# Value matmuls as side-by-side column tiles with VectorE sums in the last two tiles, and softmax reciprocals as powers of -1 on GpSimd

## The chip, the cores and the metric

The kernel runs on the eight NeuronCores of one Trainium2 chip, each core computing one of eight batch entries with the same program. The metric is the device time in microseconds of the slowest core. An execution is in a *fast* or a *slow* state: in the slow one the cores of one die or of both get a lower clock for TensorE and the time is some per cent longer, whatever the kernel. "Same" means a difference under 2%.

## The reference

A two-layer decoder trunk of width 1024 over 4096 positions. Each layer has a half-step SwiGLU feed-forward network (FFN), a mixing layer, and a second FFN. The mixing layer of layer 0 is a gated recurrence; that of layer 1 is causal attention with a learned forget gate, and both run 4 heads of cross-attention into 256 memory tokens beside it. The part that matters:

```python
s = jnp.einsum('bhqd,bhkd->bhqk', qb, k, preferred_element_type=F32) * scale
s = s + cb[..., None] - cum[:, :, None, :]
s = jnp.where(key_pos[None, :] <= q_pos[:, None], s, -jnp.inf)
p = jax.nn.softmax(s, axis=-1)
return jnp.einsum('bhqk,bhkd->bhqd', p.astype(v.dtype), v)
```

## The kernel before

The 4096 positions go in eight tiles of 512. A small scheduler inside the kernel runs at build time: it keeps a rough clock for every engine, books an assumed cost for each instruction, and picks greedily which piece of work is issued next, so attention, recurrence and norms are laid between the dense FFN matmuls. The order is then fixed; on the chip each engine takes its own queue strictly in that order and waits on semaphores. Attention of tile `t` has key blocks `0..4t+3` of 128 keys each. It does, per pair of heads and two key blocks, four score matmuls (64 rows each, two side by side), four exponentials on ScalarE, and four value matmuls whose stationary operand holds 64 columns of values and 64 columns of ones:

```python
for h2 in range(2):
    for i in range(2):
        blk = 2 * b + i
        p, q0 = ps_[2 * i + h2], q0s[i]
        self.mm(o[h2], o[h2].ap[:, q0:TT], vb.ap[:, blk % 8, h2:h2 + 2, :].rearrange("p a d -> p (a d)"),
                p.ap[:, q0:TT], blk == 0, blk == nkb - 1, [vb, p], signal=True)
```

The ones give the softmax denominator, copied 64 times, as the other half of the output. At the end of a head pair the denominators are inverted on VectorE in four pieces of 128 columns and multiplied with the values:

```python
def softmax_end(self, o, cat, c):
    dn, nu = self.F.get(), self.F.get()
    # ... four copies out of PSUM: values to nu, denominators to dn
    def recip(j):
        r = slice(128 * j, 128 * j + 128)
        self.fw.op("dve", lambda e, a=dn.ap[:, r]: e.reciprocal(a, a), reads=[dn], writes=[dn], cost=(None, 950.0))
    def end():
        cat[c] = self.Bp.get()
        self.tt("dve", cat[c], nu, dn, ALU.mult)
        self.F.put(dn, nu)
    return [(dn, lambda j=j: recip(j)) for j in range(4)] + [(nu, end)]
```

`cat` is what the output projection multiplies. `cost=(None, 950.0)` is what the scheduler books, in nanoseconds. The cross-attention of both layers uses the same ending, so there are (6 + 2) x 8 + 2 x 8 = 80 endings and 320 reciprocals.

## Time and profile before

| | before |
|---|---|
| time, two runs | 5461.5 us (fast), 5554.8 us (slow) |
| slowest core in the profile | 5459.7 us |
| TensorE on the chain that ended last | 87% |
| VectorE / ScalarE / GpSimd busy | 50% / 49% / 15% |
| mean granted TensorE clock | 0.98 to 0.99 |

The page cuts the span in 40 slices and gives the busy share of each in tenths. These are the rows of TensorE and GpSimd before:

```profile
PE   7898999999999999999999999999999999999999
...
POOL 1223120120211112210121012001200101001100
```

TensorE is nearly full from the second tenth on, and GpSimd has plenty of room. That room is what the second half of the change wants to use.

### The profile page before, as it was taken

Reading aid. Unit: us, or ns where it says so; the run is one execution under the profiler, and the core shown is the slowest. Engines: PE = TensorE matmul, PEld = TensorE weight load, DVE = VectorE, ACT = ScalarE, POOL = GpSimd, SP = SyncE. Lnnn points to the kernel's source line nnn. Section 1 sums busy time; section 2 is a strip of 40 time slices with the busy share of each in tenths; the row PEclk is TensorE's granted clock in tenths of the full one; section 3 lists DMA queues with packets and bytes.
Section 4 is the critical chain, followed back from the end, with each engine's and each line's share of the span. In section 5 each row is a group of like instructions: output and inputs, shape, how many; then the busy total and the mean of one; then the engine's idle time right before and its main releaser. Section 6 shows DMA issues by size and latency. Waiting matters only on the chain.

```text
span 5459.7 us, 84254 instructions; the slowest of 8 cores (5418.8 to 5459.7 us)
## 1 busy us (share of the span) xinstructions
PE 5252.4 (96%) x24835; PEld 2278.5 (42%) x24835; DVE 2730.0 (50%) x4101; ACT 2697.6 (49%) x4468; POOL 828.3 (15%) x1098
## 2 busy tenths in 40 slices
PE   7898999999999999999999999999999999999999
PEld 3443444444444443444434443444334444433344
DVE  4466643465545465635564455354544434443342
ACT  2356431344524365425672577246763656466641
POOL 1223120120211112210121012001200101001100
PEclk9999999999999997999999999999999999999999
DMA  8964687955795643455445443454435445555445
GB/s 180 218 170 126 143 207 175 224 141 169 167 223 181 181 127 112 147 162 146 137 134 174 144 140 115 138 169 134 135 112 189 146 146 158 184 158 169 152 148 161
DMA packets 302148, 866.23 MB, mean 159 GB/s; under 512 B 33680, under 2 KB 53264, under 8 KB 301712
## 3 DMA queue, kind: packets, MB, share of 16 engines
q1 hardware_dynamic: 275328, 775.47, 45.0%
q0 software_dynamic: 26384, 85.38, 10.3%
q8 instruction: 221, 3.62, 0.3%
q14 instruction: 215, 1.76, 0.1%
HBM read 819.72 MB, written 125.30 MB: 173 GB/s over the span
## 4 chain that ended last, share of the span: by engine, by line
PE 87%; DMA 5%; DVE 2%; ACT 2%; issue 2%; POOL 1%; SPq 1%; DVEq 0%; ACTq 0%; POOLq 0%
PE ps L652 87%; DMA sb_w<-wts 2%; DVE sb_f L686 1%; ACT sb_b L661 1%; DMA sb_f<-x 1%; ACT sb_f L661 1%; DMA wbf<-sb_w 1%; DVE sb_b L686 1%; SPq L221 1%; DMA sb_w<-wbf 1%; ACT L661 0%; POOL sb_f L669 0%; POOL sb_b L669 0%; DVE sb_b L669 0%; DVE sb_f L669 0%
## 5 line engine op out<-in xcount | busy, mean ns | idle before, releaser
L652 PE MATMUL ps<-sb_b,sb_w 128*128 128x512 bf16 x19728 | 4464.5, 383 | 83.9 <-DVE sb_f L686 27.0
L652 PEld LDWEIGHTS ps<-sb_b,sb_w 128*128 128x128 bf16 x19728 | 1909.2, 98 | 2513.6 <-issue 378.1
L661 ACT ACTIVATE sb_b<-ps,sb_nct 128x512 bf16<-128x512 f32 x1344 | 810.9, 691 | 342.6 <-PE ps L652 340.9
L661 ACT ACTIVATE sb_f<-ps 128x512 f32<-128x512 f32 x752 | 448.6, 597 | 1057.4 <-PE ps L652 1013.0
L686 DVE SCALAR_TENSOR_TENSOR sb_f<-sb_f,ps 128x512 f32<-128x512 f32 x704 | 481.4, 684 | 877.7 <-ACT sb_f L661 733.7
L686 DVE SCALAR_TENSOR_TENSOR sb_f<-ps,sb_f 128x512 f32<-128x512 f32 (+3 forms) x688 | 370.6, 574 | 889.0 <-PE ps L652 878.1
L669 DVE TENSOR_TENSOR sb_b<-sb_f,ps 128x512 bf16<-128x512 f32 x704 | 484.3, 688 | 287.8 <-PE ps L652 247.5
L669 POOL TENSOR_TENSOR sb_f<-sb_f 128x512 f32<-128x512 f32 (+1 forms) x282 | 360.9, 1280 | 1511.1 <-ACT sb_f L661 1506.7
L661 ACT ACTIVATE sb_f<-sb_f 128x512 f32<-128x512 f32 (+1 forms) x598 | 367.2, 625 | 415.3 <-DVE sb_f L686 248.2
L652 PE MATMUL ps<-sb_b,sb_vst 128*128 128x512 bf16 (+1 forms) x1728 | 428.9, 369 | 16.4 <-ACT sb_b L661 10.0
L669 POOL TENSOR_TENSOR sb_f<-sb_f,sb_cf 128x128 f32<-128x128 f32 x384 | 180.0, 485 | 1539.5 <-DVE sb_f L686 1532.8
L661 ACT ACT_TABLE_LOAD x172 | 220.7, 1283 | 227.4 <-PE ps L652 220.2
L661 ACT ACTIVATE sb_b<-sb_f,sb_nct 128x128 bf16<-128x128 f32 (+3 forms) x384 | 193.3, 555 | 243.6 <-POOL sb_f L669 242.7
L694 ACT COPY sb_f<-ps 128x512 f32<-128x512 f32 (+2 forms) x434 | 251.9, 582 | 114.7 <-PE ps L652 80.6
L962 DVE RECIPROCAL sb_f<-sb_f 128x128 f32<-128x128 f32 x320 | 302.2, 947 | 11.5 <-DVE sb_f L962 0.5
L686 DVE SCALAR_TENSOR_TENSOR sb_b<-sb_f,sb_vecs 128x512 bf16<-128x512 f32 (+1 forms) x392 | 286.4, 778 | 35.0 <-ACT sb_f L661 34.9
L652 PE MATMUL ps<-sb_b,sb_kst 64*128 64x512 bf16 (+1 forms) x1728 | 263.8, 368 | 22.8 <-DVE sb_f L686 9.0
L652 PEld LDWEIGHTS ps<-sb_b,sb_vst 128*128 128x128 bf16 x1728 | 160.4, 98 | 236.8 <-issue 79.7
L661 ACT ACTIVATE sb_b<-ps 128x512 bf16<-128x512 f32 (+1 forms) x258 | 143.1, 600 | 100.7 <-PE ps L652 100.5
L221 POOL DMA_DIRECT2D sb_w<-wts x179 | 97.0, 543 | 575.1 <-PE ps L652 446.6
L698 DVE COPY sb_f<-ps 64x512 f32<-64x512 f32 x160 | 109.7, 686 | 137.0 <-ACT sb_f L694 82.0
L669 DVE TENSOR_TENSOR sb_f<-ps,sb_f 128x512 f32<-128x512 f32 x128 | 88.5, 691 | 149.2 <-PE ps L652 149.2
(69 smaller groups left out, 1767.9 us busy)
## 6 DMA issues: line engine op xcount, KB each, us to landing
sb_w<-wbf SPq DMA_DIRECT2D x761, 512.0 KB, 4.1
sb_w<-wbf SPq DMA_DIRECT2D x424, 352.0 KB, 3.1
sb_w<-wts POOLq DMA_DIRECT2D x115, 512.0 KB, 9.6
wbf<-sb_w SPq DMA_DIRECT2D x113, 512.0 KB, 9.4
sb_vst<-vcache SPq DMA_DIRECT2D x96, 384.0 KB, 3.8
sb_kst<-kcache SPq DMA_DIRECT2D x96, 256.0 KB, 4.3
sb_w<-wts POOLq DMA_DIRECT2D x64, 352.0 KB, 9.6
wbf<-sb_w SPq DMA_DIRECT2D x64, 352.0 KB, 7.1
```

Source lines behind the costliest of these rows:

```text
L221: eng.dma_start(out=item[1], in_=item[2]).then_inc(item[3], 16)
L652: self.fw.op("pe", lambda e: e.matmul(out_ap, lhsT, rhs, start=start, stop=stop, skip_group_check=True), reads=reads, writes=[ps], signal= ...
L661: self.fw.op("act", lambda e: e.activation(o, i, func, **kw), reads=[in_b] + list(extra), writes=[out_b], cost=(func, ns))
L669: self.fw.op(eng, lambda e: e.tensor_tensor(o, a, b, op), reads=[a_b, b_b], writes=[out_b], cost=(None, 155 + 1.042 * n if eng == "dve" el ...
L686: self.fw.op("dve", lambda e: e.scalar_tensor_tensor(o, a, scalar, b, op0, op1), reads=[in0_b, in1_b] + list(extra), writes=[out_b], cost= ...
L694: fn, ns = (lambda e: e.copy(o, i)), 160 + 0.833 * n
L698: fn, ns = (lambda e: e.tensor_copy(o, i)), 155 + (1.042 if in_b.psum else 0.53) * n
L962: self.fw.op("dve", lambda e, a=dn.ap[:, r]: e.reciprocal(a, a), reads=[dn], writes=[dn], cost=(None, 950.0))
```

## The change

The intent is twofold. First, half of each value matmul is spent on ones. In the last two tiles (`SUMS = (6, 7)`), which are the longest, the ones go: the two heads' 64-column value matmuls run side by side in the two halves of the array, and VectorE adds the exponentials up itself. Second, VectorE then has more to do, so the reciprocals leave it, as `x ** -1` on GpSimd. The core of the diff, with cuts:

```diff
+    def inverse(self, b, r):
+        a = b.ap[:, r]
+        n = self.neg.ap.to_broadcast([128, self.width(a)])
+        self.fw.op("pool", lambda e: e.tensor_tensor(a, a, n, ALU.pow), reads=[b, self.neg], writes=[b], shared=True,
+                   cost=(None, 1500.0))
...
         def recip(j):
-            r = slice(128 * j, 128 * j + 128)
-            self.fw.op("dve", lambda e, a=dn.ap[:, r]: e.reciprocal(a, a), reads=[dn], writes=[dn], cost=(None, 950.0))
+            self.inverse(dn, slice(128 * j, 128 * j + 128))
...
+    def attn_sums(self, t, h, res, nxt):
...
+                        self.tt("dve", ac, p0, p, ALU.add, o=ac.ap[:, q0:TT], a=p0.ap[:, q0:TT], b=p.ap[:, q0:TT])
...
+                    self.mm(o, o.ap[64 * h2:64 * h2 + 64, q0:TT], vb.ap[:, blk % 8, 2 * h2, :], p.ap[:, q0:TT], blk == 0,
+                            blk == nkb - 1, [vb, p], signal=h2 == 1, tile=(128, 64, 0, h2))
...
+    SUMS = (6, 7)
```

The rest keeps the scheduler's books: eight places of the array in place of four, a model of the SBUF interface that VectorE and GpSimd share, other step counts. These alter the order of instructions from the first tiles on.

More of the change, by code (lines that the diff above doesn't have):

```diff
@@ L55, in reset @@
         self.free = 0.0
-        self.quad = [0.0] * 4
+        self.quad = [0.0] * 8
         self.mode = None
@@ L61, in reset @@
         self.busy = 0.0
+        self.port = collections.deque(maxlen=8)
 HOP = 100.0
@@ L120, in _deps, with _port, _run @@
         return at
-    def _run(self, q, at, cost):
+    def _port(self, q, at, ns):
+        for a, b in self.q["pool" if q.name == "dve" else "dve"].port:
+            if a - 50.0 <= at < b:
+                at = b
+        q.port.append((at, at + ns))
+        return at
+    def _run(self, q, at, cost, shared=False):
         if q.is_pe:
             n, rows, cols, r, c = cost
-            quads = [2 * i + j for i in ((0, 1) if rows == 128 else (r,)) for j in ((0, 1) if cols == 128 else (c,))]
+            w = cols // 32
+            quads = [4 * i + j for i in ((0, 1) if rows == 128 else (r,)) for j in range(w * c, w * c + w)]
             if (rows, cols) != q.mode:
-                before = max(q.quad) + (92.0 if q.mode else 0.0)
+                before = max(q.quad) + (100.0 if q.mode else 0.0)
             else:
@@ L148, in _run @@
             start += 1300.0
+        if shared:
+            start = self._port(q, start, ns)
         q.busy += ns
@@ L154, in pe_free, with op @@
         return max(self.q["pe"].quad)
-    def op(self, qname, fn, reads=(), writes=(), signal=True, cost=(None, 600.0)):
+    def op(self, qname, fn, reads=(), writes=(), signal=True, cost=(None, 600.0), shared=False):
         q = self.q[qname]
-        end = self._run(q, self._deps(q, reads, writes), cost)
+        end = self._run(q, self._deps(q, reads, writes), cost, shared)
         if signal:
@@ L293, in __init__ @@
         self.n = n
+        self.every = name[:4] != "attn"
         self.count = 0
@@ L345, in step @@
     def step(self, lane):
-        self.count += 1
+        self.count += 1 if lane.need.units or self.every else 0
         self.units += lane.need.units
@@ L512, in whole @@
         for k in range(8):
-            yield Need(self.h[k], f=2, lag=(("act", 700.0),))
+            yield Need(self.h[k], f=2, b=k // 7, lag=(("act", 700.0),))
             self.add(k)
@@ L572, in _tensors @@
         t["ones"] = sb("ones", [128, 128], F32)
+        t["neg"] = sb("neg", [128, 1], F32)
         t["vecs"] = sb("vecs", [128, self.vc["_n"]], F32)
@@ L605, in _bufs @@
         self.ones = B(t["ones"], "ones")
+        self.neg = B(t["neg"], "neg")
         self.vecs = B(t["vecs"], "vecs")
@@ L669, in tt @@
         self.fw.op(eng, lambda e: e.tensor_tensor(o, a, b, op), reads=[a_b, b_b], writes=[out_b],
-                   cost=(None, 155 + 1.042 * n if eng == "dve" else 190 + 2.11 * n))
+                   shared=eng == "pool" or not (a_b.psum or b_b.psum), cost=(None, 155 + 1.042 * n if eng == "dve" else 190 + 2.11 * n))
     def ts(self, eng, out_b, in_b, s1, s2, op0, op1, o=None, i=None, extra=()):
@@ L686, in stt @@
         self.fw.op("dve", lambda e: e.scalar_tensor_tensor(o, a, scalar, b, op0, op1),
-                   reads=[in0_b, in1_b] + list(extra), writes=[out_b], cost=(None, ns))
+                   reads=[in0_b, in1_b] + list(extra), writes=[out_b], shared=not (in0_b.psum or in1_b.psum), cost=(None, ns))
     def copy(self, eng, out_b, in_b, o=None, i=None):
@@ L698, in copy @@
             fn, ns = (lambda e: e.tensor_copy(o, i)), 155 + (1.042 if in_b.psum else 0.53) * n
-        self.fw.op(eng, fn, reads=[in_b], writes=[out_b], cost=(None, ns))
+        self.fw.op(eng, fn, reads=[in_b], writes=[out_b], shared=eng == "pool", cost=(None, ns))
     WRITE_AT = (1,)
@@ L884, in ffn @@
         if nxt:
-            yield Need(h[7], f=1)
+            yield Need(h[7], f=1, b=1)
             nxt.add(7)
@@ L1016, in out_proj @@
         if nxt:
-            yield Need(h[7], f=1)
+            yield Need(h[7], f=1, b=1)
             nxt.add(7)
@@ L1406, in attn, with load, drop, adds @@
         yield from self.out_proj(1, h, cat, nxt)
+    def attn_sums(self, t, h, res, nxt):
+        fw = self.fw
+        qT, qmn = res["q"][0:6], res["q"][6:8]
+        nkb = 4 * t + 4
+        nb = nkb // 2
+        chunks = [(c, j) for c in range(6) for j in range((nkb + 7) // 8)]
+        where = {x: i for i, x in enumerate(chunks)}
+        kv = {}
+        def load(i):
+            if i >= len(chunks):
+                return
+            c, j = chunks[i]
+            n = min(8, nkb - 8 * j)
+            kb, vb = self.kst.next(), self.vst.next()
+            tiles = range(2 * j, 2 * j + n // 4)
+            fw.dma("sp", kb.ap[:, 0:n * 128], self.kc_d[c, :, j * 1024:j * 1024 + n * 128],
+                   reads=[self.kc_bufs[(c, i)] for i in tiles], writes=[kb], kb=32 * n)
+            fw.dma("sp", vb.ap[:, 0:n].rearrange("p t a d -> p t (a d)"), self.vc_d[c, :, 8 * j:8 * j + n, :],
+                   reads=[self.vc_bufs[(c, i)] for i in tiles], writes=[vb], kb=48 * n)
+            kv[(c, j)] = (kb, vb)
+        load(0)
+        load(1)
+        cat = [None] * 8
+        pend, fins, live, factors, halves, scaled = [], [], {}, {}, {}, set()
+        state = {"qk": 0, "pv": 0, "done": 0}
+        sums, used = collections.deque(), collections.Counter()
+        def drop(pool, *bufs):
+            for x in bufs:
+                used[id(x)] += 1
+                if used[id(x)] == 2:
+                    del used[id(x)]
+                    pool.put(x)
+        def adds():
+            for _ in range(6 * nb):
+                yield Need(cond=lambda: bool(sums))
+                c, b, ps_, q0s = sums.popleft()
+                if b == 0:
+                    yield Need(f=2)
+                    acc = [self.F.get() for _ in range(2)]
+                elif b == 2 * t:
+                    for h2 in range(2):
+                        ec = factors[c][h2]
+                        yield Need(ec, lag=(("dve", self.LAG),))
+                        self.tt("dve", acc[h2], acc[h2], ec, ALU.mult)
+                        drop(self.F, ec)
+                for i in range(2):
+                    for h2 in range(2):
+                        p, q0, ac = ps_[2 * i + h2], q0s[i], acc[h2]
+                        if b == 0 and i == 0:
+                            continue
+                        p0 = ps_[h2] if b == 0 else ac
+                        yield Need(p, lag=(("dve", self.LAG),))
+                        self.tt("dve", ac, p0, p, ALU.add, o=ac.ap[:, q0:TT], a=p0.ap[:, q0:TT], b=p.ap[:, q0:TT])
+                        if b == 0 and q0:
+                            self.copy("dve", ac, p0, o=ac.ap[:, 0:q0], i=p0.ap[:, 0:q0])
+                        drop(self.Bp, p, *([p0] if b == 0 else []))
+                state["done"] += 1
+                if b == nb - 1:
+                    ends_of(c, acc)
+        def ends_of(c, x):
+            got = halves.setdefault(c, [])
+            got.append(x)
+            if len(got) == 2:
+                fins.append((c, *sorted(got, key=lambda y: isinstance(y, list))))
+        def scale(c):
+            o, ec = live[c], factors[c]
+            for h2 in range(2):
+                r = slice(64 * h2, 64 * h2 + 64)
+                self.tt("dve", o, o, ec[h2], ALU.mult, o=o.ap[r, :], a=o.ap[r, :], b=ec[h2].ap[r, :])
+            drop(self.F, *ec)
+            scaled.add(c)
+        def values(c, b, ps_, q0s, vb):
+            if b == 0:
+                live[c] = self.PS.get()
+            o = live[c]
+            for i in range(2):
+                blk, q0 = 2 * b + i, q0s[i]
+                for h2 in range(2):
+                    p = ps_[2 * i + h2]
+                    self.mm(o, o.ap[64 * h2:64 * h2 + 64, q0:TT], vb.ap[:, blk % 8, 2 * h2, :], p.ap[:, q0:TT], blk == 0,
+                            blk == nkb - 1, [vb, p], signal=h2 == 1, tile=(128, 64, 0, h2))
+            drop(self.Bp, *ps_)
+            state["pv"] += 1
+            if b == nb - 1 or b % 4 == 3:
+                load(where[(c, (2 * b) // 8)] + 2)
+            if b == nb - 1:
+                ends_of(c, live.pop(c))
+        def ripe():
+            c, b, ps_, _, vb = pend[0]
+            if b and b == 2 * t:
+                return False
+            now = fw.pe_free() - HOP
+            bufs = [*ps_, vb, *([live[c]] if b else ())]
+            return max(x.there() for x in bufs) <= now and (b > 0 or self.PS.room(5) <= now)
+        def products():
+            while state["pv"] < 6 * nb:
+                yield Need(cond=lambda: bool(pend) or state["pv"] == 6 * nb)
+                if not pend:
+                    continue
+                c, b, ps_, _, vb = pend[0]
+                if b and b == 2 * t and c not in scaled:
+                    scale(c)
+                n = int(b == 0)
+                yield Need(vb, *ps_, *([live[c]] if b else ()), ps=n, units=2)
+                if pend and pend[0][0:2] == (c, b):
+                    values(*pend.pop(0))
+        def scores():
+            for c in range(6):
+                cq = []
+                for b in range(nb):
+                    db = b - 2 * t
+                    if db == 0:
+                        ec = factors[c] = []
+                        for h2 in range(2):
+                            yield Need(self.c3, ps=1, f=2, lag=(("act", 1500.0),), units=1)
+                            x = self.PS.get()
+                            self.mm(x, x.ap, self.sel(2 * c + h2), self.c3.ap, True, True, [self.cb, self.c3])
+                            q = self.F.get()
+                            self.copy("act", q, x)
+                            cq.append(q)
+                            self.PS.put(x)
+                            if t > 0:
+                                e_ = self.F.get()
+                                self.act(AF.Exp, e_, q)
+                                ec.append(e_)
+                    while (c, (2 * b) // 8) not in kv:
+                        yield Need(cond=lambda: (c, (2 * b) // 8) in kv)
+                    kb, vb = kv[(c, (2 * b) // 8)]
+                    yield Need(kb, qT[c], *cq, ps=4, b=4, f=2 if db >= 0 else 0, lag=(("act", 1800.0),),
+                               cond=lambda: state["qk"] - state["done"] < 4 and state["qk"] - state["pv"] < 3, units=2)
+                    if pend and ripe():
+                        values(*pend.pop(0))
+                    q0s, ss, ps_ = [], [], []
+                    for i in range(2):
+                        diag = 2 * b + i - 4 * t
+                        q0 = 128 * diag if diag > 0 else 0
+                        q0s.append(q0)
+                        k0 = ((2 * b + i) % 8) * 128
+                        for h2 in range(2):
+                            b0 = 64 * h2
+                            s = self.PS.get()
+                            ss.append(s)
+                            self.mm(s, s.ap[:, q0:TT], kb.ap[b0:b0 + 64, k0:k0 + 128], qT[c].ap[b0:b0 + 64, q0:TT], True,
+                                    True, [kb, qT[c]], tile=(64, 128, h2, 0))
+                    for i in range(2):
+                        blk, q0 = 2 * b + i, q0s[i]
+                        for h2 in range(2):
+                            hh = 2 * c + h2
+                            s = ss[2 * i + h2]
+                            bias = self.nct.ap[:, blk, hh:hh + 1]
+                            p = self.Bp.get()
+                            if db < 0:
+                                self.act(AF.Exp, p, s, scale=0.125, bias=bias, extra=[self.nct])
+                            else:
+                                tm = self.F.get()
+                                self.stt(tm, s, 0.125, cq[h2], ALU.mult, ALU.add, o=tm.ap[:, q0:TT],
+                                         a=s.ap[:, q0:TT], b=cq[h2].ap[:, q0:TT])
+                                self.tt("pool", tm, tm, self.cf, ALU.add, o=tm.ap[:, q0:q0 + 128],
+                                        a=tm.ap[:, q0:q0 + 128], b=self.tri)
+                                self.act(AF.Exp, p, tm, o=p.ap[:, q0:TT], i=tm.ap[:, q0:TT], bias=bias, extra=[self.nct])
+                                self.F.put(tm)
+                            self.PS.put(s)
+                            ps_.append(p)
+                    pend.append((c, b, ps_, q0s, vb))
+                    sums.append((c, b, ps_, q0s))
+                    state["qk"] += 1
+                    if b == nb - 1:
+                        self.F.put(*cq)
+                        self.Bp.put(qT[c])
+        def ends():
+            for _ in range(6):
+                yield Need(cond=lambda: bool(fins))
+                c, o, acc = fins.pop(0)
+                yield Need(o, f=1, lag=(("act", 1000.0),))
+                nu = self.F.get()
+                self.copy("act", nu, o)
+                self.PS.put(o)
+                parts = []
+                for h2 in range(2):
+                    yield Need(acc[h2], b=2, lag=(("dve", 500.0),))
+                    hi, lo = self.Bp.get(), self.Bp.get()
+                    self.copy("dve", hi, acc[h2])
+                    self.tt("dve", lo, acc[h2], hi, ALU.subtract)
+                    self.F.put(acc[h2])
+                    parts += [hi, lo]
+                yield Need(*parts, ps=1, f=1, units=2)
+                d = self.PS.get()
+                for i in range(2):
+                    for h2 in range(2):
+                        x = parts[2 * h2 + i]
+                        self.mm(d, d.ap[64 * h2:64 * h2 + 64, :], self.ones_b[:, 0:64], x.ap, i == 0, i == 1,
+                                [self.ob, x], signal=True, tile=(128, 64, 0, h2))
+                self.Bp.put(*parts)
+                dn = self.F.get()
+                self.copy("act", dn, d)
+                self.PS.put(d)
+                for j in range(4):
+                    yield Need(dn, lag=(("dve", 300.0),))
+                    r = slice(128 * j, 128 * j + 128)
+                    self.inverse(dn, r)
+                yield Need(b=1, lag=(("dve", 300.0),))
+                cat[c] = self.Bp.get()
+                self.tt("dve", cat[c], nu, dn, ALU.mult)
+                self.F.put(dn, nu)
+        yield Fork(ends(), adds(), products(), scores(), self.cross(qmn, cat))
+        yield from self.out_proj(1, h, cat, nxt)
@@ L1432, in _prologue @@
         fw.op("dve", lambda e: e.memset(self.ob.ap, 1.0), writes=[self.ob], cost=tiny)
+        fw.op("dve", lambda e: e.memset(self.neg.ap, -1.0), writes=[self.neg], cost=tiny)
         fw.op("dve", lambda e: e.memset(self.ones.ap, 1.0), writes=[self.ones], cost=tiny)
@@ L1498 @@
     HELD = 3
+    SUMS = (6, 7)
+    LAG = 1800.0
     PARKED = (2, 3, 4, 5, 6)
@@ L1555, in make @@
                 n = None if t in parked else norm("b2", t)
-                yield from self.attn(t, H[t], RES[t], n)
+                yield from (self.attn_sums if t in self.SUMS else self.attn)(t, H[t], RES[t], n)
                 if n:
```

## The prediction

> **What bounds the kernel now.** I read the page's busy table and chain first, then the waits of TensorE, then the timeline of TensorE inside an attention stretch, then the busy table of the two stretches that the change rewrites.
>
> ```profile
> PE 5252.4 (96%) x24835; PEld 2278.5 (42%) x24835; DVE 2730.0 (50%) x4101; ACT 2697.6 (49%) x4468; POOL 828.3 (15%) x1098
> ...
> PE ps L652 87%; DMA sb_w<-wts 2%; DVE sb_f L686 1%; ACT sb_b L661 1%; DMA sb_f<-x 1%; ACT sb_f L661 1%; DMA wbf<-sb_w 1%; DVE sb_b L686 1%; SPq L221 1%; DMA sb_w<-wbf 1%; ACT L661 0%; POOL sb_f L669 0%; POOL sb_b L669 0%; DVE sb_b L669 0%; DVE sb_f L669 0%
> ...
> L962 DVE RECIPROCAL sb_f<-sb_f 128x128 f32<-128x128 f32 x320 | 302.2, 947 | 11.5 <-DVE sb_f L962 0.5
> ```
>
> The page says that matmuls set the end: 87% of the chain is TensorE. Busy alone would not prove it, since matmuls overlap, but the chain and the short waits do. The 320 reciprocals cost VectorE 302 us and stand nowhere in the chain.
>
> The timeline of TensorE inside the attention of the last tile shows the price of each piece:
>
> ```profile
> 4903.76 3.63 PE L652 MATMUL ps<-sb_b,sb_w 128*128 128x512 bf16 x16
> 4907.23 1.03 PE L652 MATMUL ps<-sb_b,sb_vst 128*128 128x512 bf16 x4
> 4908.19 0.60 PE L652 MATMUL ps<-sb_b,sb_kst 64*128 64x512 bf16 x4
> 4908.72 3.63 PE L652 MATMUL ps<-sb_b,sb_w 128*128 128x512 bf16 x16
> ```
>
> The first column is the start. Sixteen dense matmuls take 4907.23 - 4903.76 = 3.47 us, so 0.217 us each. Four value matmuls (sb_vst) then fill 0.96 us: 4 x 0.217 = 0.868, and 0.09 is left for the step from whole-array to half-row matmuls. Four score matmuls (sb_kst, 64 rows) fill 0.53 us: two pairs side by side, 2 x 0.217 = 0.434, and 0.096 for the step back. So a change of array shape costs about 0.095 us, half-array pairs cost one matmul, and one step of attention with its dense filling lasts 4.96 us with no wait in it.
>
> The two attention stretches which will change, by the first and last value matmul of the last two tiles, are about 4240 to 4668 us and 4785 to 5264 us. Their busy table, columns being the stretch, its length, then PE, PEld, DVE, ACT and POOL busy with counts, the granted clock, the DMA share and GB/s:
>
> ```profile
> 4230.00:4670.00 440.00, 436.76 (x2146) 178.46 (x2144) 177.37 (x273) 280.61 (x479) 56.40 (x74) 1.00 0.49 151
> 4770.00:5266.00 496.00, 489.31 (x2394) 198.12 (x2393) 193.86 (x298) 313.36 (x533) 48.59 (x69) 1.00 0.51 161
> ```
>
> TensorE is idle there for 3 and 7 us, VectorE is 40% and 39% busy, the clock is full. Every matmul removed here should come off the end, as long as VectorE can take its new work.
>
> **What the Trainium skill says.** "TensorEngine Tiling (Array Packing)", Key Properties: changing the tiling mode drains TensorE. The trace agrees, with the 0.095 us above; Gotcha 2 of that page adds that column tiling excludes fast weight load, which no run of this kernel shows yet. "TensorE: Matmul & The Clock Gate", Part 3, gives 2.38x for three column tiles, so column packing does run side by side; the trace has only row pairs, which reach about 2x before the switch. "VectorE: DVE Perf Modes", the errata section, has (N+151)/0.96 ns for an fp32 tensor_tensor, 691 ns at N=512; the lines below have 684 to 692 as medians. "GPSIMD Engine Reference", Specifications, says that GpSimd shares its SBUF interfaces with VectorE and contends with VectorE instructions that have two SBUF inputs. The VectorE rows of the add/multiply helper agree (min/median/max ns):
>
> ```profile
> L669 DVE TENSOR_TENSOR sb_b<-sb_f,ps x704: 686/689/690, 32.2 to 5418.3; 128x512 bf16<-128x512 f32 x176
> ...
> L669 DVE TENSOR_TENSOR sb_b<-sb_f x82: 629/692/1719, 19.4 to 5281.5; 128x512 bf16<-128x512 f32 x82
> ...
> L669 DVE TENSOR_TENSOR sb_b<-sb_f,sb_b x48: 679/692/1779, 292.6 to 3937.9; 128x512 bf16<-128x512 f32 x48
> ```
>
> With one input in PSUM all 704 lie within 686 to 690 ns; with both in SBUF the median is the same and the longest is 1.7 to 1.8 us.
>
> **The change part by part.**
>
> *TensorE, removed.* Before, each value matmul carries 64 columns of values and 64 of ones, which give the softmax denominator. In the last two tiles the ones go, and the two heads' 64-column matmuls stand side by side. Tiles 6 and 7 have 28 and 32 key blocks, 6 head pairs, 2 heads: 720 value matmuls, by the order of the built program 648 of 512 columns and 24 each of 384, 256 and 128, which is 648 + 24 x 1.5 = 684 full ones. Halved: 342 x 0.217 = 74.2 us less. The denominators come back as 4 small-output matmuls per head pair, 48 in all, paired: 24 x 0.217 = 5.2 us more. Net 318 x 0.217 = 69.0 us.
>
> *TensorE, added.* Values (128 rows, 64 columns), scores (64 rows) and dense are now three shapes, so a step that was values, scores, dense with two changes of shape has three. In the order of the built program the changes of shape rise from 915 to 1164, nearly all of it in the last two tiles (166 to 278 and 190 to 321). 249 x 0.095 = 23.7 us. So the stream on TensorE shrinks by 69.0 - 23.7 = 45.3 us. Per step: 16 x 0.217 + 2 x 0.217 + 2 x 0.217 + 3 x 0.095 = 4.63 us against 4.96.
>
> *VectorE, added in the last two tiles.* Per head pair 4 adds in each of 14 or 16 steps less 2: 324 adds in tile 6 and 372 in tile 7. Of these 12 each per tile are 384, 256 and 128 wide. At 0.69 us for 512 (0.55, 0.42, 0.28 for the narrow ones, from the scaling rows of the same widths): tile 6 is 288 x 0.69 + 15 = 214 us, tile 7 is 336 x 0.69 + 15 = 247 us. Splitting the sums in a high and low part is 12 copies and 12 subtractions, 13 us per tile; 12 copies out of PSUM leave and 12 half-size scalings come, which cancel. Twenty-eight reciprocals leave each stretch, 27 us. So VectorE goes from 177 to 177 + 214 + 13 - 27 = 377 us in a stretch of some 420, and from 194 to 427 us in one of some 475: 90% in both, from 40%. Back to back VectorE instructions start some 0.61 us apart in the timeline though each lasts 0.69, so a bit more room is left than 90% says.
>
> *Reciprocals.* 320 leave VectorE (302 us over the span) and 320 powers come to GpSimd. No row of the trace has a power; the change books 1.5 us for each, against 456 ns for the plain 128-wide addition there. Taken at that, GpSimd gains 480 us and goes to about 1310 us, 24% of the span: no bound. Outside the last two tiles VectorE is not what TensorE waits for in sum (TensorE's waits for the FFN's scaling there are 38 us in all), so this frees little: I book 0 to 5 us.
>
> *Contention.* In a changed stretch GpSimd gets 28 powers, 42 us, on top of 50: busy about 22% of the time. If an add meets it in 22% of cases and waits half of a 1 us operation, that is about 0.1 us for each of 324 or 372 adds, some 35 us, and VectorE is at 97 or 98%. So it becomes nearly a second bound. Adds go in front of FFN operations in a strict queue, and those free the PSUM banks. I book 15 us of new TensorE waits over both stretches.
>
> Sum: 5461 - 45 + 15 = 5431 us in the fast state.
>
> **The rivals.** First, *VectorE takes over*: contention or the in-place sums make it the bound, and TensorE waits in the last two tiles grow by 50 us or more; the result is 5460 to 5500. For it speak the 90% and the 1.7 us maxima; against it, the adds wait for nothing but the exponentials and have slack of several steps. Second, *the column pairs don't run side by side*, or their weight loads show: all 342 stay, the switches are paid, 5461 + 24 + 5 = 5490. Against it: the row pairs pack well, and a weight load of 98 ns is well hidden behind 217. Third, *all goes through*: VectorE keeps up, the freed reciprocals remove some early waits: 5400. Fourth, *reshuffling*: the order is chosen greedily and already differs in the first tiles, before the new code runs; TensorE's waits, 199 us in all by the list of waits, could move by 20 us either way.
>
> **Range and chances.** I take 5430 us. The low end, 5385, is the full 45 us plus some 30 from reshuffling and freed VectorE. The high end, 5490, covers the first two rivals, and a median that has a slow run in it: before has one fast run (5461) and one of 5555. A gain of 2% would need 109 us, more than the 69 that the removed matmuls hold; a loss of 2% would need all of the gain lost and 110 us of stalls on top. So faster 0.02, same 0.94, slower 0.04.
>
> **What would show it.** Right: value matmuls of the last tiles as 128*64 with pairs of pairs in about 0.53 us (with the switch), steps near 4.6 us, VectorE near 90% in both stretches, adds with a median near 0.69 us and a tail past 1.5, powers near 1.5 us, TensorE waits for VectorE there of 10 to 30 us. Wrong: four value matmuls still taking near 0.96 us; switches well above 0.1 us; powers of 3 us or more, which would hold VectorE by the shared interface; or TensorE waits of over 50 us in the last two tiles.

## The result

| | before | changed |
|---|---|---|
| time, two runs | 5461.5 (fast), 5554.8 (slow) | 10945.5, 11036.0 (both fast) |
| ratio of fast runs | 1 | 2.017 (95%: 1.995 to 2.039) |
| GpSimd busy | 828 us, 15% | 7456 us, 68% |
| mean granted TensorE clock | 0.98 to 0.99 | 0.74 to 0.75 |

The ratios are formed from fast runs of both kernels, so they aren't quite the ratios of the times that are quoted: the means above give 10990.7 / 5461.5 = 2.012. The changed kernel takes twice the time. These lines are from its page: the busy table, the chain by line, and the group of the powers.

```profile
PE 5561.7 (50%) x24883; PEld 2310.7 (21%) x24883; DVE 2888.1 (26%) x4526; ACT 2688.8 (24%) x4462; POOL 7456.0 (68%) x1418
...
POOL sb_f L969 50%; PE ps L667 33%; DVE sb_f L701 1%; POOL sb_f L684 1%; ACT sb_b L676 1%; ACT sb_f L676 0%; DMA sb_w<-wts 0%; DMA sb_f<-x 0%; ACT sb_f L709 0%; DVE sb_b L684 0%; DVE sb_f L684 0%; POOL sb_b L711 0%; POOL sb_b L684 0%; DMA sb_w<-wbf 0%; DVE sb_b L701 0%
...
L969 POOL TENSOR_TENSOR sb_f<-sb_f,sb_neg 128x128 f32<-128x128 f32 x320 | 6639.5, 20750 | 761.2 <-ACT sb_f L709 737.9
```

Line 969 is the power. Before, no GpSimd line had more than 1% of the chain; now this one has half of it. One power takes 20.75 us, not the 1.5 us that the change books for it, and 320 of them are 6640 us. The instruction view gives minimum, median and maximum:

```profile
L969 POOL TENSOR_TENSOR sb_f<-sb_f,sb_neg x320: 20705/20717/21277, 315.6 to 10839.4; 128x128 f32<-128x128 f32 x160
```

The minimum and the median are 12 ns apart, so it is no outlier, and what runs beside it can matter little; a run below tests a power by itself.

How does GpSimd, an engine off the critical path, stop TensorE? The timelines of one spot in tile 6 show it. First GpSimd (start, length, what):

```profile
9023.07 42.07 POOL L969 TENSOR_TENSOR sb_f<-sb_f,sb_neg 128x128 f32<-128x128 f32 x2 [15.02 <-ACT sb_f L709]
```

Then VectorE in the same time:

```profile
9036.99 4.29 DVE L684 TENSOR_TENSOR sb_f<-sb_f,sb_b 128x512 f32<-128x512 f32 x7
...
9042.83 1.28 DVE L684 TENSOR_TENSOR sb_f<-sb_f,sb_b 128x512 f32<-128x512 f32 x2
9106.96 0.69 DVE L684 TENSOR_TENSOR sb_b<-sb_f 128x512 bf16<-128x512 f32 x1 [62.84 <-POOL sb_f L969]
...
9109.37 0.68 DVE L701 SCALAR_TENSOR_TENSOR sb_f<-sb_f,ps 128x512 f32<-128x512 f32 x1
```

And TensorE:

```profile
9025.07 3.63 PE L667 MATMUL ps<-sb_b,sb_w 128*128 128x512 bf16 x16
9028.63 0.62 PE L667 MATMUL ps<-sb_b,sb_vst 128*64 128x512 bf16 x4
9029.18 0.61 PE L667 MATMUL ps<-sb_b,sb_kst 64*128 64x512 bf16 x4
9029.72 3.63 PE L667 MATMUL ps<-sb_b,sb_w 128*128 128x512 bf16 x16
...
9049.19 0.60 PE L667 MATMUL ps<-sb_b,sb_kst 64*128 64x512 bf16 x4
9110.31 2.29 PE L667 MATMUL ps<-sb_b,sb_w 128*128 128x512 bf16 x5 [60.51 <-DVE sb_f L701]
```

There are three things to see. While the powers run, VectorE's sums go on at 0.6 us each. Counted in the whole trace, 212 of the 600 full-width sums lie wholly inside a power, and the longest of them takes 0.89 us: a power doesn't hold VectorE through the shared SBUF interface. GpSimd's additions of 512 columns (1.3 us each) do: all 16 sums over 1 us (up to 1.76) overlap one of these and end about 0.55 us after it. TensorE's step is what was hoped for: from 9025.07 to 9029.72, 4.65 us, with the four value matmuls as 128*64 tiles in 0.55 us. Then at 9044 VectorE reaches the multiplication that needs the finished powers, and stands there for 62.84 us. The FFN's scaling (line 701), which frees PSUM for TensorE, is behind it in the queue, and TensorE stops for 60.51 us. The first five matmuls after that take 2.29 us. Five of the same form in the first experiment below, without a stall before them, take 1.24 us:

```profile
4859.64 1.24 PE L667 MATMUL ps<-sb_b,sb_w 128*128 128x512 bf16 x5
```

The Trainium skill, "TensorE: Matmul & The Clock Gate", Part 1, says that TensorE falls to half its clock after an idle window of about 3.4 us. The trace agrees: the clock granted after this stall is 0.50 in each microsecond up to 9113 and 1.00 from 9114 on. So a stall costs more than its own length.

The list of waits (who waited for what: us in total, times, longest) sums this up:

```profile
DVE sb_b L684 <- POOL sb_f L969: 4871.0, 80, 86.2
PE ps L667 <- DVE sb_f L701: 3100.4, 87, 79.5
```

All 80 multiplications wait, one for each ending. GpSimd's causal masks stand behind powers too: in the same list ScalarE's exponentials wait 1056 us for them.

### The profile page after: what moved, and what is told of

Its sections match the earlier page's. It is cut to its first block, busy times and chain, and to the rows that moved or that the text cites. A ratio compares the mean times of both kernels' runs of the same rounds, so it can differ in the third digit from the quotient of the medians.

```text
span 11034.5 us, 86614 instructions; the slowest of 8 cores (10921.9 to 11034.5 us)
## 1 busy us (share of the span) xinstructions
PE 5561.7 (50%) x24883; PEld 2310.7 (21%) x24883; DVE 2888.1 (26%) x4526; ACT 2688.8 (24%) x4462; POOL 7456.0 (68%) x1418
## 4 chain that ended last, share of the span: by engine, by line
POOL 52%; PE 33%; issue 10%; DVE 2%; ACT 1%; DMA 1%; SPq 0%; DVEq 0%; POOLq 0%; ACTq 0%
POOL sb_f L969 50%; PE ps L667 33%; DVE sb_f L701 1%; POOL sb_f L684 1%; ACT sb_b L676 1%; ACT sb_f L676 0%; DMA sb_w<-wts 0%; DMA sb_f<-x 0%; ACT sb_f L709 0%; DVE sb_b L684 0%; DVE sb_f L684 0%; POOL sb_b L711 0%; POOL sb_b L684 0%; DMA sb_w<-wbf 0%; DVE sb_b L701 0%
## 5 line engine op out<-in xcount | busy, mean ns | idle before, releaser
L969 POOL TENSOR_TENSOR sb_f<-sb_f,sb_neg 128x128 f32<-128x128 f32 x320 | 6639.5, 20750 | 761.2 <-ACT sb_f L709 737.9
L667 PE MATMUL ps<-sb_b,sb_w 128*128 128x512 bf16 x19728 | 4746.4, 399 | 2587.4 <-DVE sb_f L701 1286.4
L667 PEld LDWEIGHTS ps<-sb_b,sb_w 128*128 128x128 bf16 x19728 | 1963.4, 102 | 5241.3 <-issue 3423.2
L684 DVE TENSOR_TENSOR sb_b<-sb_f 128x512 bf16<-128x512 f32 x82 | 66.1, 806 | 4871.4 <-POOL sb_f L969 4871.0
L667 PE MATMUL ps<-sb_b,sb_vst 128*128 128x512 bf16 (+3 forms) x1728 | 380.8, 388 | 306.2 <-ACT sb_b L676 284.3
L684 DVE TENSOR_TENSOR sb_f<-sb_f,sb_b 128x512 f32<-128x512 f32 (+4 forms) x722 | 454.5, 681 | 6.2 <-DVE sb_b L713 1.2
L667 PEld LDWEIGHTS ps<-sb_b,sb_kst 64*128 64x128 bf16 x1728 | 61.4, 95 | 1596.9 <-issue 1593.1
L667 PE MATMUL ps<-sb_b,sb_cb 128*128 128x512 bf16 (+2 forms) x357 | 109.2, 405 | 268.0 <-POOL sb_b L684 237.4
```

What stands on the lines that cost most here:

```text
L667: self.fw.op("pe", lambda e: e.matmul(out_ap, lhsT, rhs, start=start, stop=stop, skip_group_check=True), reads=reads, writes=[ps], signal= ...
L684: self.fw.op(eng, lambda e: e.tensor_tensor(o, a, b, op), reads=[a_b, b_b], writes=[out_b], shared=eng == "pool" or not (a_b.psum or b_b.p ...
L969: self.fw.op("pool", lambda e: e.tensor_tensor(a, a, n, ALU.pow), reads=[b, self.neg], writes=[b], shared=True, cost=(None, 1500.0))
```

## The experiments

The theory after reading this, called P: the power's own duration is the whole loss. Its rivals: S, the sums or the third array shape cost the time; C, the power is long only through contention or through its in-place form; B, it is long only through the stride-0 exponent (one value broadcast over all columns). The diffs are against the changed kernel and show the lines that matter, with cuts.

### Sums kept, reciprocals back on VectorE

```diff
-        self.fw.op("pool", lambda e: e.tensor_tensor(a, a, n, ALU.pow), ..., cost=(None, 1500.0))
+        self.fw.op("dve", lambda e: e.reciprocal(a, a), reads=[b], writes=[b], cost=(None, 950.0))
```

> The changed kernel with one part undone: the reciprocals go back to VectorE (320 of 947 ns), the column values, the VectorE sums and everything else stay. Theory P (the power instruction's own 20.7 us is the whole loss, by occupying GpSimd and by holding VectorE's queue behind it): the time falls from 10991 to 5400 to 5470 us, a ratio of 0.99 to 1.00 to the kernel before, and the value matmuls of the last two tiles keep their 4.65 us step. Rival S (the sums on VectorE or the third array shape cost the time): it stays above 6000 us.

Measured: fast runs of 5422.8, 5422.9 and 5424.4 us, ratio 0.9972 (0.9951 to 0.9994) to the kernel before. So the whole loss goes with the powers, and S falls. The two attention stretches in the busy table of this run (stretch, length, then PE, PEld, DVE, ACT, POOL busy, clock, DMA share, GB/s):

```profile
4230.00:4660.00 430.00, 423.83 (x2169) 159.37 (x2166) 376.49 (x603) 276.55 (x472) 61.17 (x75) 1.00 0.49 153
4790.00:5240.00 450.00, 440.87 (x2283) 163.44 (x2281) 405.51 (x662) 302.61 (x516) 42.92 (x62) 1.00 0.54 168
```

VectorE is 88% and 90% busy, and even so TensorE is idle for only 6 and 9 us.

### The powers alone, without the sums

```diff
-    SUMS = (6, 7)
+    SUMS = ()
```

> The changed kernel with the other part undone: the old attention in all eight tiles, the powers on GpSimd kept. Theory P: 10500 to 11200 us, GpSimd over 60% busy, the power rows still 20.7 us. Rival S: close to the kernel before, 5460 us.

Measured: 11236.9 us, one fast run; the 320 powers have the same median, 20717 ns, and 49% of the chain. This is the same loss from the other side.

### Neither: only the new order

Both edits above together.

> Both parts undone: old attention, reciprocals on VectorE; only the scheduler's new bookkeeping (shared interface model, 8 column places, step counts, the extra page asked for) is left. Theory P: same work as the kernel before in a slightly other order, 5430 to 5490 us, ratio 0.995 to 1.005. If the reordering by itself matters: outside of that. The difference of this run to the run with sums and reciprocals is what the column values gain, by my step 45 us less the new waits.

Measured: fast runs of 5441.9 to 5457.4 us, ratio 1.0019 (1.0003 to 1.0035). The new order by itself gains nothing; it costs about 10 us, with an interval of 2 to 19. Against this run, the sums with VectorE reciprocals gain 0.0047 of 5439 us, 26 us.

### The power by itself

The kernel before, with these after its last store, three times over. They are written short here, one line for each instruction and not as the file has them (`x` is an exponential of the input, `neg` a broadcast -1, `m` a tile of -1, `one` a broadcast 1):

```diff
+ L1720 pool tensor_tensor(y[:, 0:128], x[:, 0:128], neg, mult)
+ L1721 pool tensor_tensor(y[:, 0:128], x[:, 0:128], neg, pow)
+ L1722 pool tensor_tensor(y[:, 0:128], x[:, 0:128], m[:, 0:128], pow)
+ L1723 pool tensor_tensor(y[:, 0:512], x[:, 0:512], neg, pow)
+ L1724 pool tensor_tensor(y[:, 0:32], x[:, 0:32], neg, pow)
+ L1725 pool tensor_tensor(y[0:16, 0:128], x[0:16, 0:128], neg, pow)
+ L1726 pool tensor_tensor(y[:, 0:128], x[:, 0:128], one, pow)
+ L1727 pool tensor_tensor(y[:, 0:128], one, neg, pow)
+       dve  reciprocal of 128 and of 512 columns
```

> The kernel before, followed after its last store by instructions on an otherwise idle core, three times each: GpSimd product 128x128, power 128x128 with a broadcast exponent (as in the change), with a dense exponent tile, 512 wide, 32 wide, on 16 partitions, with exponent +1, with base 1, and VectorE reciprocals 128 and 512 wide. Theory P: every 128-wide power takes about 20.7 us with nothing beside it, 512 wide about 83 us, 32 wide about 5.2 us, independent of the values; the 16-partition one also about 20.7 us if each lane group works alone. Rival C (it is long in the changed kernel only by contention with VectorE or by the in-place form): about 1.5 us here. Rival B (the stride-0 exponent is at fault): the dense form is several times shorter. The total time grows by the probes' sum, some 600 us.

Measured: 6032.9 us in all. The groups of these lines (busy us, mean ns of one):

```profile
L1723 POOL TENSOR_TENSOR sb_f<-sb_f 128x512 f32<-128x512 f32 x3 | 245.8, 81917 | 0.4
...
L1722 POOL TENSOR_TENSOR sb_f<-sb_f 128x128 f32<-128x128 f32 x3 | 62.3, 20772 | 0.4
L1721 POOL TENSOR_TENSOR sb_f<-sb_f 128x128 f32<-128x128 f32 x3 | 62.2, 20728 | 0.4
L1726 POOL TENSOR_TENSOR sb_f<-sb_f,sb_ones 128x128 f32<-128x128 f32 x3 | 62.2, 20726 | 0.4
L1725 POOL TENSOR_TENSOR sb_f<-sb_f 16x128 f32<-16x128 f32 x3 | 62.1, 20716 | 0.4
...
L1724 POOL TENSOR_TENSOR sb_f<-sb_f 128x32 f32<-128x32 f32 x3 | 16.2, 5415 | 0.4
...
L1720 POOL TENSOR_TENSOR sb_f<-sb_f 128x128 f32<-128x128 f32 x3 | 1.2, 399 | 161.6 <-ACT sb_f L661 161.3
```

On an idle core, out of place, with a dense exponent, with exponent +1 or on 16 partitions, 128 columns take 20.7 us; C and B fall. From 32 to 512 columns the time grows by 81.92 - 5.42 = 76.5 us, so 159 ns per column and some 0.3 us fixed. The product of the same shape takes 0.40 us, a fiftieth. VectorE's reciprocal took 0.953 us for 128 columns and 3.353 us for 512.

### The power at the booked length

```diff
-        a = b.ap[:, r]
+        a = b.ap[:, r.start:r.start + 8]
```

> Wrong result on purpose: the changed kernel with each power cut from 128 to 8 columns, all else and the whole order of instructions the same. By the probe (5.42 us at 32 columns, 20.72 at 128, so 159 ns per column and 0.3 us fixed) such a power takes about 1.6 us, near the 1.5 us that the change and my prediction booked. If the prediction failed in that one term alone, this run gives what it forecast: 5400 to 5450 us, ratio 0.993 to 1.002, with GpSimd near 24% busy. If another step was wrong too, it stays above 5490 us, the top of the range.

Its output is wrong, which doesn't matter for the time. The booked cost is unchanged, so the order of instructions is that of the changed kernel. Measured: fast runs of 5450.6 to 5470.5 us, ratio 1.0019 (0.9955 to 1.0083). The powers:

```profile
L969 POOL TENSOR_TENSOR sb_f<-sb_f,sb_neg x320: 1624/1642/2207, 309.4 to 5283.7; 128x8 f32<-128x8 f32 x160
```

Nothing but the width of this instruction was changed, and the time falls from 10991 us into the predicted range. The four fast runs have a mean of 5461 us, which is still 30 us above the predicted 5431 and 37 us above the run with VectorE reciprocals. As a ratio, the prediction was 5431 / 5461 = 0.9945, and the interval here begins at 0.9955: the predicted gain just misses it. In its profile VectorE's multiplication still waits 122 us for the powers, and two cores were granted a clock of 0.95 between 600 and 1400 us where the others had 0.98 to 0.99. Most of the 37 us lies before tile 6, whose first value matmul comes at 4238 to 4279 us on the eight cores, against 4225 to 4238 us with VectorE reciprocals. How the rest splits is open.

### A quarter of the powers

```diff
+        if r.start < 384:
+            self.fw.op("dve", lambda e: e.reciprocal(a, a), reads=[b], writes=[b], cost=(None, 950.0))
+            return
```

> The changed kernel, but only the last of the four column groups of each denominator goes to GpSimd (80 powers, 1657 us there in place of 6630); the other three are VectorE reciprocals, which run first. If the loss is in proportion to GpSimd's time: 5423 + 5570/4, about 6800 us. If there is slack that hides a 20 us power per head pair: under 5900 us. If each power that stands alone still delays what waits behind it by its full length: about 5423 + 1657, 7080 us.

Measured: one fast run, 6769.9 us (two slow ones of 7048 and 7461). That is 6770 - 5423 = 1347 us for 80 powers, 16.8 us each; with all 320 it is (10991 - 5423) / 320 = 17.4 us each. This is the first of the three expectations, a loss in proportion to GpSimd's time. GpSimd is only 37% busy here, so this isn't an engine that is full: each power delays the rest by some four fifths of its own length.

### Two cures with all powers

In the first, the multiplication goes to GpSimd, so that VectorE waits for no power; in the second, the scheduler books the true cost; the third is both.

```diff
-            self.tt("dve", cat[c], nu, dn, ALU.mult)
+            self.tt("pool", cat[c], nu, dn, ALU.mult)
```
```diff
-                   cost=(None, 1500.0))
+                   cost=(None, 20717.0))
```

> The changed kernel with its slow powers, but the multiplication by the reciprocal, which waits for the powers, runs on GpSimd in place of VectorE (80 of about 1.3 us more there, 0.69 us less each on VectorE). Theory H (most of the loss is VectorE's strict queue held by that multiplication: 4871 us of waits for the powers): those waits vanish and the end comes from GpSimd's own work of some 7560 us: 7600 to 9000 us. Rival G (the powers' chain itself, through the output projection and GpSimd's other work, sets the end either way): 10300 us or more.

> The changed kernel with one number changed: the scheduler books 20717 ns for a power in place of 1500. Theory B (a wrong booking made the schedule blind, and a right one hides a good part): 7600 to 9500 us, as GpSimd's total of 7450 us is a floor that no order can go under. Rival: the order matters little, since VectorE's multiplication still stands behind the powers in its queue: 10000 us or more.

> The last two cures together: the multiplication on GpSimd and 20717 ns booked for a power. Either alone gave about 10200 us. If the two losses (VectorE's queue held, and an order made for a 1.5 us power) are separate: 8000 to 9500 us, towards the floor of 7550 us of GpSimd work. If what is left is GpSimd's own queue, in which the norm sums and the causal mask stand behind the powers whatever the order: 9500 to 10200 us.

Measured, one fast run each: 10261.8, 10161.5 and 9915.2 us. The first two expectations of my theory missed widely. VectorE's waits for the powers did vanish in the first, and only 730 us went: GpSimd is 74% busy by now, and others wait for what is behind the powers in its queue. From the first run's list of waits:

```profile
ACT sb_b L676 <- POOL sb_f L684: 2127.4, 114, 156.6
PE ps L667 <- POOL sb_b L684: 1309.2, 36, 168.1
DVE sb_f L701 <- POOL sb_b L684: 891.1, 19, 90.8
```

ScalarE's exponentials wait for the causal masks twice as long as in the changed kernel (1056 us), and TensorE waits 1309 us for GpSimd's bf16 results, which are norm sums and the moved multiplication (237 us in the changed kernel). Nor was VectorE's queue freed: the FFN's scaling now waits 891 us for these same results. The third run fits the rival in its text, 9500 to 10200.

### The same two ways with a quarter of the powers

With 80 powers GpSimd has room, so the two ways can be told apart. One run takes the quarter and moves the multiplication to GpSimd; the other keeps it on VectorE, books the true cost and lets the multiplication into the queue only when the power is due to be done. The lines that do this last part:

```diff
-        return [(dn, lambda j=j: recip(j)) for j in range(4)] + [(nu, end)]
+        return [(dn, lambda j=j: recip(j)) for j in range(4)] + [(dn, end)]
...
-                yield Need(b=1, lag=(("dve", 300.0),))
+                yield Need(dn, b=1, lag=(("dve", 300.0),))
```

> 80 powers (one column group of four), and the multiplication by the reciprocal on GpSimd, so that VectorE waits for no power. Way (a), VectorE's queue held: of the 1350 us that the 80 powers cost, most goes: 5450 to 5900 us. Way (b), GpSimd's own queue (norm sums and masks behind the powers): 6300 us or more.

> 80 powers, booked with their true 20717 ns, and the multiplication stays on VectorE but is put into its queue only when the power is due to be done. Way (a): 5450 to 5900 us, and the wait of VectorE's multiplication for the powers falls from 1520 us to under 400. Way (b): 6300 us or more, as GpSimd's queue is the same.

Measured: the first fell in the slow state (6418 us at best), so only the cores of its less disturbed die can be used, 6105 to 6120 us at a clock of 0.93; the second was fast, 6172.7 us. This is between the two expectations. VectorE's waits for the powers, in the quarter run and then in the one with the late multiplication:

```profile
DVE sb_b L684 <- POOL sb_f L972: 1521.5, 79, 26.3
```
```profile
DVE sb_b L684 <- POOL sb_f L972: 377.6, 33, 32.8
```

Taking three quarters of VectorE's wait away recovers 6770 - 6173 = 597 of the 1347 us; in the other run VectorE waits for no power at all, and some 6770 - 6113 = 657 us are recovered. Both runs change the order or the load of GpSimd as well, so "VectorE's queue carries about half of the delay" is an estimate. The other half stays in both. GpSimd's own queue is a likely way: ScalarE's exponentials wait 542 us for the masks in the late run and 475 us in the other, against 394 us in the plain quarter run and 248 us with no powers. No run took that wait away, so this part is argued and not shown.

### What the column values and the adds are worth

```diff
+                        if b == 0 or b >= 2 * t:
                             self.tt("dve", ac, p0, p, ALU.add, ...)
```

> Wrong result on purpose: as the run with sums and VectorE reciprocals, but the VectorE additions of the steps between the first and the diagonal ones are left out (some 44 of 54 adds per head pair in tile 6, 52 of 62 in tile 7). It shows what the column values alone are worth. Theory (my sum of the prediction): TensorE alone gains about 43 us against the order-only run, so a ratio of 0.993 to 0.995 to the kernel before, and TensorE's waits in the two stretches fall to under 8 us. If the adds cost nothing: the same as with them, 0.997.

Measured, with a wrong result: fast runs of 5404.8, 5407.4, 5410.3 and 5460.5 us, ratio 0.9965 (0.9907 to 1.0023). The interval can't tell this from the run with all adds. The three lower runs agree within 6 us and lie 13 to 20 us under all fast runs of that one (5422.8 to 5424.4), with the kernel before at 5432 to 5441 us in both but for two fast runs of 5455 and 5482. They point to some 40 us for the column values alone (5448, the median of the order-only run's fast runs, less 5407), and some 16 us that the adds take back.

The traces give a sharper figure. Take the stretch from the first value matmul of tile 6 to the last of tile 7, at full clock, on the slowest core (the others lie within 4 us). The order-only run and this one have the same other work in it (3312 dense matmuls) and need 1013 and 976 us: the column values are worth 38 us. The run with all adds has 56 more dense matmuls there, 12 us; without these it takes 995 - 12 = 983 us, so the adds take back about 7 us. TensorE is idle for 15 us of the stretch with the adds, for 6 us without them and for 8 us in the order-only run.

### Further: three tiles, and wider reciprocals

> Reciprocals back on VectorE, and the column values with VectorE sums in the last three tiles in place of two. By the count of the built program the matmul stream falls by another 123 full matmuls, 26.7 us, and 89 more changes of shape cost some 9 us: 17 us less if VectorE keeps up, ratio to the kernel before about 0.994. If VectorE's load is the limit in the third tile too: no better than the run with two tiles, 0.997 or above.

Edit: `SUMS = (5, 6, 7)`, reciprocals on VectorE. Measured: fast runs of 5428.8, 5433.8 and 5464.9 us, ratio 0.9997 (0.9948 to 1.0046). The third tile brings nothing that shows.

> A candidate to beat both kernels: the column values and sums in the last two tiles, with one VectorE reciprocal of 512 columns (3.35 us by the probe) in place of four of 128 (3.81 us and the gaps between them). It saves 80 x 0.46 = 37 us of VectorE, some 7 us of it in the two full stretches, but holds the queue 3.4 us at a time. Theory: VectorE's time is worth little outside of the two stretches, so 5410 to 5430 us, ratio 0.995 to 0.999; if the longer hold shows, worse than with four, over 0.999.

Edit: as the first experiment, with one reciprocal of 512 columns in place of four, and a cost of 3360 booked for it.

```diff
-            self.inverse(dn, slice(128 * j, 128 * j + 128))
+            self.inverse(dn, slice(0, TT))
...
-        return [(dn, lambda j=j: recip(j)) for j in range(4)] + [(nu, end)]
+        return [(dn, lambda j=j: recip(j)) for j in range(1)] + [(nu, end)]
```

Measured: fast runs of 5411.7, 5412.5, 5413.7, 5434.9 and 5455.4 us, ratio 0.9956 (0.9900 to 1.0012). Its three best runs are the lowest with a right result, below the 5435 us of the best run of the kernel before in the same call. The interval touches 1, so it is likely, and not shown, that this one beats the kernel before. The first experiment, which keeps the change's first half and leaves four reciprocals on VectorE, does beat it, by 0.3% (0.1 to 0.5).

## Why the prediction was wrong

The prediction was 5430 us in 5385 to 5490, with 0.04 for slower; measured was 10991 us.

**The step that failed** is the one on reciprocals: "the change books 1.5 us for each ... Taken at that, GpSimd gains 480 us and goes to about 1310 us, 24% of the span: no bound." The text itself says that no row of the trace has a power. The 1500 ns in the diff is what its author let the scheduler assume, and I took it for a duration. Measured, the term is 320 x 20.75 = 6640 us, fourteen times as much. "No bound" failed with it: every multiplication waits for its powers in VectorE's queue, 4871 us in all. That this one term makes the loss is shown twice: with the power cut to 1.6 us the time is in the range, and with VectorE's reciprocals it is 5423 us. What it doesn't explain is some 30 to 40 us by which the run with short powers misses the predicted gain.

**The rivals** were all about VectorE, the packing and the order; none let the unmeasured instruction be long. Its length stood only in the last paragraph ("powers of 3 us or more, which would hold VectorE by the shared interface"), a sign that came true but had no share in the chances. The mechanism given there was wrong as well: sums run at 0.6 us beside a power. The power holds VectorE through the multiplication in its queue, by the estimate above about half of the delay at 80 powers, and the rest comes by another way, likely GpSimd's queue.

**TensorE, removed and added** was right in kind and a little high. Predicted 4.63 us per step and about 0.53 us for four value matmuls; measured 4.65 and 0.55. The trace of the changed kernel has 1163 changes of shape against 914, as counted beforehand (1164 and 915); the few matmuls of 12 rows count as whole-array. They cost 0.09 to 0.13 us and not 0.095, and the 45 us are 38 in the run without adds. The weight loads of the 64-column tiles are longer, 108 ns against 98 ns, and stay hidden.

**VectorE's load** was predicted too high: 377 and 427 us, 90% of both stretches, with the reciprocals gone. In the run with short powers, which has them gone, it is 345 us of 420 (82%) and 400 us of 470 (85%). With the reciprocals still there it is 88% and 90%. The adds were booked at 0.69 us, and one among others takes 0.61 us of VectorE's time. The 35 us of contention with the powers don't show either: a full-width sum takes 715 ns on average in the run with short powers and 724 ns in the one with none. The long adds that the prediction saw are real, but they come from GpSimd's additions of 512 columns. (The 684 ns that it gives for "the lines below" stands in a row that it leaves out; the rows shown have 689 to 692.)

**The 15 us of new waits** are some 7 to 10 us: with the adds TensorE is idle for 15 us of the stretch of tiles 6 and 7, against 8 us in the order-only run and 6 us without the adds.

**The gain of freed reciprocals**, "0 to 5 us", didn't show even at the booked length: the run with 1.6 us powers isn't faster than the one with VectorE's reciprocals.

**Reordering**, "20 us either way", came out at about +10 us.

## What to carry to other kernels

A cost written in a scheduler or in a diff is an assumption; where the trace has no row of that instruction, time it by itself before anything rests on it, or give the case that it is many times longer a share in the chances. An engine that is mostly idle is still no free place for a slow instruction: look for what waits for its result, and for what stands behind that in strict queues. In the run with 80 powers GpSimd was 37% busy and each slow instruction still cost four fifths of its length.

## What the Trainium skill lacked or had wrong

- "GPSIMD Engine Reference" has no cost for a power: it takes 159 ns per column and some 0.3 us, 20.72 us for 128 columns, the same on 16 partitions as on 128 and the same for every exponent tried; a product of the same shape takes 0.40 us.
- The same page (Specifications) says that GpSimd contends with VectorE instructions with two SBUF inputs, and makes no difference between GpSimd's own instructions. Here it holds for additions of 512 columns, beside which such a sum takes up to 1.76 us, and not for powers: of 212 sums inside a power of 20.7 us none took over 0.89 us.
- "TensorEngine Tiling (Array Packing)" (Key Properties) has the drain at a change of tiling mode, without a figure: it is 0.09 to 0.13 us here, in every direction between 128x128, 64-row and 64-column tiles that the timelines show.
- "VectorE: DVE Perf Modes" describes the reciprocal's iterations and gives no time: 0.953 us for 128 fp32 columns and 3.353 us for 512.
